# Scores of the chunked linear attention: one matmul per head on its own 32 rows and PSUM bank, in place of block-diagonal queries

## Chip, cores and metric

One core of a Trainium2 chip runs the whole program. The metric is device time in microseconds (us) of one execution; lower is better. Three executions of the kernel before gave 1266.64, 1267.24 and 1271.37 us, median 1267.24 us.

## The reference, cut to what matters

Two token groups (512 prompt tokens, 1024 sample tokens) go through one layer: modulated RMSNorm, an input projection, four mixers side by side, a gate, an output projection, a norm and a residual add. The change lies in one mixer, the gated linear attention (GLA) with 4 heads of 32 key columns and 64 value columns, run forwards and backwards:

```python
def gla_chunked(q, k, v, g, strict):
    # o_t = sum_{s<=t} (q_t * prod_{r=s+1..t} a_r) . k_s  v_s,  a = exp(g), per head
    ...
    decay = jnp.exp(jnp.where(mask[:, :, None], diff, -jnp.inf))
    scores = jnp.einsum('bhtd,bhsd,bhtsd->bhts', qi, ki, decay)
    intra = jnp.einsum('bhts,bhsv->bhtv', scores, vi)
    ...

o_f = gla_chunked(q, k, v, log_gate(lr_f, wg2_f, bg_f), strict=False)
o_b = flip(gla_chunked(flip(q), flip(k), flip(v), flip(log_gate(lr_b, wg2_b, bg_b)), strict=True))
o = rms_norm(o_f + o_b, onorm_g)
```

All is float32 to a tight tolerance, so a product of two operands is taken as three matmuls on the parts high and low of each (h*h, h*l, l*h), in the type float32r.

## The kernel before, in words

The 1536 tokens are three groups of 512: group 2 is the prompt, groups 0 and 1 the sample. For each group `jobs` runs the input projection as many matmuls over weights that stream in (SyncE queue), are split into a high part on ScalarE (ACT, L259) and a low part on GpSimd (POOL, L83), and are used by TensorE (PE) into the PSUM tiles `ps_mm`. These projections, the gate path and the output projection are given a late priority (`later`), and the scheduler of the tile framework, which fixes the order of every engine's instructions when the program is built, places them between the work of the mixers. So the order on each engine follows from priorities and from the scheduler's own estimate of durations; no table in the kernel sets it, and on the chip it is fixed.

`gla_pass1` (L711 to L838) runs once for each group, with tokens along the free dimension and the 4 x 32 key columns on the 128 partitions. The scores within 128 tokens are built by levels m = 1, 2, 4, ..., 64: at level m, pairs of neighbouring runs of m tokens see each other, with queries (`qsi`, `qpi`) and keys (`ksx`, `kpx`) that carry the decay up to that level, so after each level those four tiles are multiplied by decay products (L86, on POOL and VectorE (DVE)). For the six levels above 1, `level` (L746) casts the keys to `kh` (ACT, L751) with the rest `kl` (POOL, L83), and the queries to `qh` (ACT, L757) with the rest `ql` (DVE, L83).

One matmul of 128 x 128 keys against the queries would sum over all four heads. So the kernel before spreads the queries block-diagonally: the tiles `qb` [128, 2 blocks, 4 heads, 128 tokens] are zero but for the head's own 32 rows, are zeroed once per group (L740), and at each level 16 copies of 32 x 256 elements fill them (8 of `qh` on ACT at L764, 8 of `ql` on DVE at L765; half of each for the first pair of blocks). Then each block of 128 tokens takes three matmuls of 512 columns (called at L771, recorded at the helper's line L80) into one of three `ps_s` banks, and DVE copies what the level's mask selects into `st` (COPY_PREDICATED of 128x512, L774; at m = 64 four copies on ACT, L776 and L777). `st` is [tokens, block, head, tokens].

After the levels, `st` is split into `sth` (ACT, L815) and `stl` (DVE, L83), and its matmuls with the values (L820, L821) and the state products follow. Over the three groups the spread is 144 copies on ACT and 144 on DVE.

The same row-group form of matmul already stands in the kernel once: the Fourier mixer has two matmuls over 32 rows (`alt` with `um`) in a chain of matmuls over 128 rows, and `ada_cols` has matmuls over 4 rows (L172).

Of the kernel before, what the change touches and what calls it, by code (L numbers as in the profile page):

```python
# [43 lines left out]
def hybrid_encoder(  # L44
# [24 lines left out]
    def ps_s(dt=F32):  # L69
        return ps.tile([128, 512], dt, tag="s", bufs=3, name="ps_s")  # L70
# [7 lines left out]
    def mms(out, terms, first=True, last=True, skip=False):  # L78
        for i, (a, b) in enumerate(terms):
            T.matmul(out, a, b, start=first and i == 0, stop=last and i == len(terms) - 1, skip_group_check=skip)  # L80
# [20 lines left out]
    S.preload_act_table_set("natural_log_exp_and_others")  # L101
    ones = const.tile([128, 128], F32, name="ones")
    V.memset(ones, 1.0)
    zero = const.tile([128, 1], F32, name="zero")
    V.memset(zero, 0.0)
    eps = const.tile([128, 1], F32, name="eps")
    V.memset(eps, EPS)

# [602 lines left out]
    def gla_pass1(pool, ppool, g, blk0, ap_all, u_f, u_b, aq, ak, vhl, ff, avx):  # L711

        qpi = ppool.tile([128, 512], F32, tag=f"qpi{g}", bufs=1, name=f"qpi{g}")
        qsi = ppool.tile([128, 512], F32, tag=f"qsi{g}", bufs=1, name=f"qsi{g}")
        ksx = pool.tile([128, 512], F32, tag="ksx", bufs=1, name="ksx")
        mul(V, qpi, aq, ff[0])
        mul(V, qsi, aq, ff[1])

        prod = pool.tile([128, 512], F32, tag="kpx", bufs=1, name="prod2")
        for i, src in enumerate((qsi, qpi)):  # L720
            qv, kv, pv = (t.rearrange("p (n two) -> p two n", two=2) for t in (src, ak, prod))
            mul(G, pv[:, i], qv[:, i], kv[:, 1 - i])
        pd = ps_o()
        for b in range(4):
            T.matmul(pd[:, 4 * b:4 * b + 4], prod[:, b * 128:(b + 1) * 128], hm, start=True, stop=True)
        own = sm.tile([128, 16], F32, tag="own", bufs=2, name="own2")
        S.copy(own, pd[:, 0:16])
        avx = avx.rearrange("p b (h d) -> p (b h) d", h=4)
        mul(V, avx, avx, own.unsqueeze(2).to_broadcast([128, 16, 64]))
        o4 = ap_all[:, blk0:blk0 + 4, :].rearrange("p b (h d) -> p (b h) d", h=4)  # L730
        add(V, o4, o4, avx)
        kpx = pool.tile([128, 512], F32, tag="kpx", bufs=1, name="kpx")
        st = pool.tile([128, 4, 4, 128], F32, tag="st", bufs=1, name="st")
        G.memset(st, 0.0)
        tf, tb = ff
        ntot = 512

        qb = [[pool.tile([128, 2, 4, 128], F32R, tag=f"qb{k}{u}", bufs=1, name="qb") for k in "hl"] for u in range(2)]
        for t in (*qb[0], *qb[1]):
            V.tensor_copy(t.rearrange("p b h t -> p (b h t)"), zero.to_broadcast([128, 1024]))  # L740

        def halves(t, m):
            v = t.rearrange("p (n two m) -> p n two m", two=2, m=m)
            return v[:, :, 0, :], v[:, :, 1, :]

        def level(li, m):  # L746
            kh = pool.tile([128, 512], F32R, tag="kh", bufs=2, name="kh")
            kl = pool.tile([128, 512], F32R, tag="kl", bufs=2, name="kl")
            for i, src in enumerate((ksx, kpx)):
                s_, h_, l_ = halves(src, m)[i], halves(kh, m)[i], halves(kl, m)[i]  # L750
                S.copy(h_, s_)  # L751
                sub(G, l_, s_, h_)
            qh = pool.tile([128, 512], F32, tag="qh", bufs=2, name="qh")
            ql = pool.tile([128, 512], F32, tag="ql", bufs=2, name="ql")
            for i, src in enumerate((qsi, qpi)):
                s_, h_, l_ = halves(src, m)[i], halves(qh, m)[i], halves(ql, m)[i]
                S.copy(halves(qh.bitcast(F32R), m)[i], s_)  # L757
                sub(V, l_, s_, h_)
            for u in range(2):
                uc = slice(u * 256, (u + 1) * 256)  # L760
                qbh, qbl = qb[u]
                for h in range(4):
                    r = slice(32 * h, 32 * h + 32)
                    S.copy(qbh[r, :, h, :], qh[r, uc].rearrange("p (b t) -> p b t", b=2))  # L764
                    V.tensor_copy(qbl[r, :, h, :], ql[r, uc].rearrange("p (b t) -> p b t", b=2))  # L765
                for i in range(2):
                    b = 2 * u + i
                    c = slice(b * 128, (b + 1) * 128)
                    pt = ps_s()
                    rh, rl = qbh[:, i].rearrange("p h t -> p (h t)"), qbl[:, i].rearrange("p h t -> p (h t)")  # L770
                    mms(pt, [(kh[:, c], rh), (kh[:, c], rl), (kl[:, c], rh)])  # L771
                    ptv = pt.rearrange("p (h t) -> p h t", h=4)
                    if m < 64:
                        V.copy_predicated(st[:, b], mk[:, li - 1, :].unsqueeze(1).to_broadcast([128, 4, 128]), ptv)  # L774
                    else:
                        S.copy(st[0:64, b, :, 64:128], ptv[0:64, :, 64:128])  # L776
                        S.copy(st[64:128, b, :, 0:64], ptv[64:128, :, 0:64])  # L777

        for li, m in enumerate(LEVELS):
            if m > 1:  # L780
                level(li, m)
            n2 = ntot // 2
            tfv, tbv = (t.rearrange("p (n two) -> p n two", two=2) for t in (tf, tb))

            def bc(t, i):
                return t[:, :, i].unsqueeze(2).to_broadcast([128, n2, m])

            q1, q2 = halves(qpi, m)
            mul(G, q2, q2, bc(tfv, 0))
            q1, q2 = halves(qsi, m)  # L790
            mul(G, q1, q1, bc(tbv, 1))
            if m == 1:
                k1, k2 = halves(ak, 1)
                mul(G, halves(ksx, 1)[0], k1, bc(tfv, 1))
                V.tensor_copy(halves(ksx, 1)[1], k2)
                V.tensor_copy(halves(kpx, 1)[0], k1)
                mul(G, halves(kpx, 1)[1], k2, bc(tbv, 0))
            else:
                k1, k2 = halves(ksx, m)
                mul(V, k1, k1, bc(tfv, 1))  # L800
                k1, k2 = halves(kpx, m)
                mul(V, k2, k2, bc(tbv, 0))
            ntf = pool.tile([128, n2], F32, tag=f"tf{n2}", bufs=1, name="ntf")
            ntb = pool.tile([128, n2], F32, tag=f"tb{n2}", bufs=1, name="ntb")
            mul(V, ntf, tfv[:, :, 0], tfv[:, :, 1])
            mul(V, ntb, tbv[:, :, 0], tbv[:, :, 1])
            tf, tb, ntot = ntf, ntb, n2
        tfin = ppool.tile([128, 2, 4], F32, tag=f"tfin{g}", bufs=1, name=f"tfin{g}")
        V.tensor_copy(tfin[:, 0, :], tf)
        V.tensor_copy(tfin[:, 1, :], tb)  # L810
        for b in range(4):
            c = slice(b * 128, (b + 1) * 128)
            sth = pool.tile([128, 4, 128], F32R, tag="kh", bufs=2, name="sth")
            stl = pool.tile([128, 4, 128], F32R, tag="kl", bufs=2, name="stl")
            S.copy(sth, st[:, b])  # L815
            sub(V, stl, st[:, b], sth)
            po = ps_o()
            pov = po.rearrange("p (h t d) -> p h t d", h=4, t=2)
            for h in range(4):
                T.matmul(pov[:, h], sth[:, h, :], vhl[:, b, h], start=True, stop=False)  # L820
                T.matmul(pov[:, h, 0, :], stl[:, h, :], vhl[:, b, h, 0, :], start=False, stop=True)  # L821
            o4 = ap_all[:, blk0 + b, :].rearrange("p (h d) -> p h d", h=4)
            for t in range(2):
                add(V, o4, pov[:, :, t, :], o4)
            for src, u in ((ksx, u_f), (kpx, u_b)):
                pt = ps_t()
                T.transpose(pt[:, 0:128], src[:, c], ident)
                kth = pool.tile([128, 128], F32R, tag="kth", bufs=2, name="kth")
                ktl = pool.tile([128, 128], F32R, tag="ktl", bufs=2, name="ktl")
                S.copy(kth, pt[:, 0:128])  # L830
                sub(V, ktl, pt[:, 0:128], kth)
                pu = ps_o()
                puv = pu[:, 0:256].rearrange("p (h d) -> p h d", h=4)
                mms(puv, [(kth, vhl[:, b, :, 0, :]), (kth, vhl[:, b, :, 1, :]), (ktl, vhl[:, b, :, 0, :])])
                for h in range(4):
                    r = slice(32 * h, 32 * h + 32)
                    S.copy(u[r, blk0 + b, :], puv[r, h, :])
        return qpi, qsi, tfin  # L838
# [521 lines left out]
```

## Time and profile before

| | us |
|---|---|
| median of 3 executions | 1267.24 |
| the profiled execution's own time | 1264.35 |
| its span, first to last instruction | 1262.5 |
| PE busy | 1115.4 (88%) |
| DVE busy | 878.2 (70%) |
| ACT busy | 723.1 (57%) |
| POOL busy | 555.3 (44%) |
| mean granted TensorE clock | 0.943 |

The profiled execution is one of its own and not one of the three. What is said per instruction or per stretch comes from it. Matmuls are pipelined, with ends that are modelled, so the time a matmul costs in a row of matmuls is read from the distance of two starts, not from its duration.

### The profile page before, as it was taken

To read this page: it belongs to the slowest core of one execution; us is meant where nothing else is said; L and a number is where in the kernel's file an instruction comes from. 1 tells how busy PE (TensorE), PEld (TensorE's weight loads), DVE (VectorE), ACT (ScalarE), POOL (GpSimd) and SP (SyncE) were. 2 spreads that over 40 slices of the span, in tenths; PEclk is the share of its full clock that TensorE was granted. 3 is DMA by queue.
4 is the path that set the end of the run, shared out by engine and by line. 5 is a ranking of instruction groups with operands and counts; after the bars stand their busy time and mean duration, and the time that the engine had idled before them with its cause. 6 is when DMAs were issued, how large, how long until landed. Compare 5 with 4: busy or idle time off the path is not lost. (4 is left out here: it accounts for less than half of the span.)

```text
span 1262.5 us, 20723 instructions
## 1 busy us (share of the span) xinstructions
PE 1115.4 (88%) x7258; PEld 977.6 (77%) x7258; DVE 878.2 (70%) x1618; ACT 723.1 (57%) x1752; POOL 555.3 (44%) x503
## 2 busy tenths in 40 slices
PE   5998798899999958898997779859999998988995
PEld 1587697685999946667897758758988987987995
DVE  6469988638443699854359996485787678787536
ACT  4354667547665437674224567634666777776653
POOL 3256536734233487334526654455242321333123
PEclk8998999889999978899998989969999999997998
DMA  8371424456223613255653123455235212145133
GB/s 311 105 221 51 143 67 136 147 186 191 79 68 95 214 43 123 65 185 177 176 163 117 51 67 125 142 167 179 73 112 198 84 59 74 45 137 164 51 110 116
DMA packets 111224, 158.43 MB, mean 125 GB/s; under 512 B 11749, under 2 KB 58309, under 8 KB 111121
## 3 DMA queue, kind: packets, MB, share of 16 engines
q1 hardware_dynamic: 110824, 157.10, 39.7%
q8 instruction: 57, 0.93, 0.3%
q14 instruction: 47, 0.38, 0.1%
q10 hardware_dynamic: 296, 0.01, 0.0%
HBM read 125.22 MB, written 31.86 MB: 124 GB/s over the span
## 5 line engine op out<-in xcount | busy, mean ns | idle before, releaser
L83 POOL TENSOR_TENSOR wl<-wr,wh 128x512 fp32r<-128x512 f32 (+1 forms) x199 | 267.1, 1346 | 397.4 <-ACT wh L259 336.0
L80 PE MATMUL ps_mm<-wl,oph 128*128 128x256 f32 x1120 | 323.9, 290 | 9.0 <-POOL wl L83 6.3
L80 PE MATMUL ps_mm<-wh,oph 128*128 128x256 f32 x1120 | 321.8, 290 | 9.7 <-ACT kev L449 4.9
L80 PE MATMUL ps_mm<-wh,opl 128*128 128x256 f32 x1120 | 321.5, 289 | 0.0
L80 PEld LDWEIGHTS ps_mm<-wl,oph 128*128 128x128 f32 x1120 | 219.5, 196 | 13.2 <-POOL wl L83 7.3
L80 PEld LDWEIGHTS ps_mm<-wh,oph 128*128 128x128 f32 x1120 | 217.6, 195 | 15.4 <-ACT kev L449 5.2
L80 PEld LDWEIGHTS ps_mm<-wh,opl 128*128 128x128 f32 x1120 | 218.7, 196 | 2.7
L259 ACT CAST wh<-wr 128x512 fp32r<-128x512 f32 (+1 forms) x216 | 131.7, 612 | 125.6 <-PE ps_mm L80 68.6
L503 DVE TENSOR_REDUCE nm<-ps_s 128x1 f32<-128x512 f32 x160 | 108.6, 685 | 56.7 <-PE ps_s L502 55.8
L83 DVE TENSOR_TENSOR ptl<-ps_t,pth 128x512 fp32r<-128x512 f32 x160 | 107.9, 683 | 46.7 <-ACT pth L520 46.2
L80 PE MATMUL ps_mm<-oph,wh 128*128 128x512 f32 x288 | 119.6, 416 | 18.8 <-ACT cev L458 10.2
L510 ACT ACTIVATE pr<-ps_s,nm 128x512 f32<-128x512 f32 x160 | 109.4, 690 | 25.5 <-DVE nm L506 25.0
L80 PE MATMUL ps_mm<-opl,wh 128*128 128x512 f32 x288 | 117.0, 406 | 0.0
L80 PE MATMUL ps_mm<-oph,wl 128*128 128x512 f32 x288 | 116.9, 407 | 0.0
L520 ACT CAST pth<-ps_t 128x512 fp32r<-128x512 f32 x160 | 91.3, 590 | 43.7 <-PE ps_t L518 42.5
L518 PE MATMUL ps_t<-cs,pr 128*128 128x128 f32 x640 | 92.3, 278 | 2.4 <-ACT pr L510 1.1
L518 PEld LDWEIGHTS ps_t<-cs,pr 128*128 128x128 f32 x640 | 76.0, 143 | 12.5 <-ACT pr L510 2.9
L765 DVE CAST qb<-ql 32x256 fp32r<-32x256 f32 x144 | 81.1, 563 | 2.9 <-PE ps_s L80 0.8
L80 PEld LDWEIGHTS ps_mm<-oph,wh 128*128 128x128 f32 x288 | 57.0, 198 | 33.2 <-ACT cev L458 11.6
L80 PE MATMUL ps_s<-qb,kh 128*128 128x512 f32 x144 | 50.2, 441 | 27.0 <-DVE st L774 22.7
L80 PEld LDWEIGHTS ps_mm<-oph,wl 128*128 128x128 f32 x288 | 56.7, 197 | 12.4
L80 PEld LDWEIGHTS ps_mm<-opl,wh 128*128 128x128 f32 x288 | 57.4, 199 | 11.5
(350 smaller groups left out, 2373.2 us busy)
## 6 DMA issues: line engine op xcount, KB each, us to landing
wr<-wp SPq DMA_DIRECT2D x152, 256.0 KB, 2.8
wr<-wo SPq DMA_DIRECT2D x60, 256.0 KB, 2.7
adar<-ada SPq DMA_DIRECT2D x16, 512.0 KB, 6.6
zT<-zr SPq DMA_DIRECT2D x30, 256.0 KB, 2.3
zt<-zT SPq DMA_DIRECT2D x30, 256.0 KB, 4.1
mt<-mixd SPq DMA_DIRECT2D x24, 256.0 KB, 4.3
xt<-x_s SPq DMA_DIRECT2D x4, 1024.0 KB, 5.5
wr<-ada SPq DMA_DIRECT2D x16, 256.0 KB, 2.8
```

Source lines behind the costliest of these rows:

```text
L80: T.matmul(out, a, b, start=first and i == 0, stop=last and i == len(terms) - 1, skip_group_check=skip)
L83: e.tensor_tensor(out, a, b, ALU.subtract)
L259: (V.tensor_copy if part_engine(HIGH_V, u, S) is V else S.copy)(h[:, 0:n], raw[:, 0:n])
L503: V.tensor_reduce(nm[:, f:f + 1], sp, AX, ALU.max, negate=True)
L510: S.activation(pr, sps[f], AF.Exp, bias=nm[:, 0:1], accum_out=rsum[:, b, h, f:f + 1])
L518: T.transpose(pt[:, k * 128:(k + 1) * 128], pr[f][:, k * 128:(k + 1) * 128], ident)
L520: S.copy(pth[f][:, :, qc], ptv)
L765: V.tensor_copy(qbl[r, :, h, :], ql[r, uc].rearrange("p (b t) -> p b t", b=2))
```

## The change

The tiles `qb`, their zeroing and all copies into them go, with the constant `zero`. `qh` and `ql` become float32r. For each of the 4 blocks and 3 terms there are now four matmuls, one for each head, of 32 rows (the head's own), 128 key columns and 128 query columns; head h writes all four blocks into its own PSUM bank: three from `ps_s` and the fourth from `ps_o`, which shares its three banks with the transposes. `st` is now ordered [tokens, head, block, tokens], so that the copy out of PSUM is one per head, of the same 128x512, and the split of `st` reads it with a stride.

```diff
-    zero = const.tile([128, 1], F32, name="zero")
-    V.memset(zero, 0.0)
...
-        qb = [[pool.tile([128, 2, 4, 128], F32R, tag=f"qb{k}{u}", bufs=1, name="qb") for k in "hl"] for u in range(2)]
-        for t in (*qb[0], *qb[1]):
-            V.tensor_copy(t.rearrange("p b h t -> p (b h t)"), zero.to_broadcast([128, 1024]))
...
-            qh = pool.tile([128, 512], F32, tag="qh", bufs=2, name="qh")
-            ql = pool.tile([128, 512], F32, tag="ql", bufs=2, name="ql")
+            qh = pool.tile([128, 512], F32R, tag="qh", bufs=2, name="qh")
+            ql = pool.tile([128, 512], F32R, tag="ql", bufs=2, name="ql")
...
-            for u in range(2):
-                uc = slice(u * 256, (u + 1) * 256)
-                qbh, qbl = qb[u]
-                for h in range(4):
-                    r = slice(32 * h, 32 * h + 32)
-                    S.copy(qbh[r, :, h, :], qh[r, uc].rearrange("p (b t) -> p b t", b=2))
-                    V.tensor_copy(qbl[r, :, h, :], ql[r, uc].rearrange("p (b t) -> p b t", b=2))
-                for i in range(2):
-                    b = 2 * u + i
-                    c = slice(b * 128, (b + 1) * 128)
-                    pt = ps_s()
-                    rh, rl = qbh[:, i].rearrange("p h t -> p (h t)"), qbl[:, i].rearrange("p h t -> p (h t)")
-                    mms(pt, [(kh[:, c], rh), (kh[:, c], rl), (kl[:, c], rh)])
-                    ptv = pt.rearrange("p (h t) -> p h t", h=4)
-                    if m < 64:
-                        V.copy_predicated(st[:, b], mk[:, li - 1, :].unsqueeze(1).to_broadcast([128, 4, 128]), ptv)
...
+            pts = [ps_s(), ps_s(), ps_s(), ps_o()]
+            for b in range(4):
+                c = slice(b * 128, (b + 1) * 128)
+                for i, (k, q) in enumerate(((kh, qh), (kh, ql), (kl, qh))):
+                    for h in range(4):
+                        r = slice(32 * h, 32 * h + 32)
+                        T.matmul(pts[h][:, c], k[r, c], q[r, c], start=i == 0, stop=i == 2)
+            for h in range(4):
+                ptv = pts[h].rearrange("p (b t) -> p b t", b=4)
+                if m < 64:
+                    V.copy_predicated(st[:, h], mk[:, li - 1, :].unsqueeze(1).to_broadcast([128, 4, 128]), ptv)
...
-            S.copy(sth, st[:, b])
-            sub(V, stl, st[:, b], sth)
+            S.copy(sth, st[:, :, b])
+            sub(V, stl, st[:, :, b], sth)
```

In the changed file the line numbers are lower by two to ten (the level's matmul is L760, its predicated copy L764). The scheduler orders the changed program anew, so other work moves too. The built programs show how, at two places.

PE, group 2, around one block's matmuls in the middle of the levels, before (`ps_s<-qb,...` is the level, `ps_mm<-...` the projections):

```order
L80 MATMUL ps_s<-qb,kh 128x512 [waits DVE_49]
L80 MATMUL ps_s<-qb,kh 128x512
L80 MATMUL ps_s<-qb,kl 128x512
L80 MATMUL ps_mm<-wl,oph 128x256
L80 MATMUL ps_mm<-wh,opl 128x256
L80 MATMUL ps_mm<-wh,oph 128x256
```

Four more projection matmuls follow before the next block's three.

PE, group 2, the end of one level and the fourth head of the next, as it stands now (x3 are the heads 0, 1 and 2 in turn; `ps_o` is head 3):

```order
L760 MATMUL ps_s<-qh,kh 128x128 x3
L760 MATMUL ps_s<-ql,kh 128x128 x3
L760 MATMUL ps_s<-qh,kl 128x128 x3
L760 MATMUL ps_o<-qh,kh 128x128 [waits Activation_49]
L760 MATMUL ps_o<-ql,kh 128x128 [waits DVE_49]
L760 MATMUL ps_o<-qh,kl 128x128 [waits Pool_49]
```

Head 3 comes first, as 12 matmuls on one row group; then stand 8 projection matmuls, then for heads 0, 1 and 2 three matmuls each that wait for DVE (their bank's copy of the level before), then 27 in turn over three heads. Between the levels there were some 30 projection matmuls per level in group 2, and there are 8 now; those that left stand after the levels.

DVE, group 0, before, four rows of the spread and what stands around them:

```order
L774 COPY_PREDICATED st<-mk,ps_s 128x512 [waits PE_49]
L774 COPY_PREDICATED st<-mk,ps_s 128x512 [waits DVE_49,PE_49]
L765 CAST qb<-ql 32x2x128 [waits DVE_49,PE_49]
L765 CAST qb<-ql 32x2x128 x3
L774 COPY_PREDICATED st<-mk,ps_s 128x512 [waits PE_49]
L86 TENSOR_TENSOR ksx<-ksx,ntf 128x16x16 [waits Pool_49]
L86 TENSOR_TENSOR kpx<-kpx,ntb 128x16x16 [waits Pool_49]
L83 TENSOR_TENSOR ql<-qsi_7107,qh 128x8x32 [waits DVE_49,Activation_49]
```

and now, at a later level of the same group (`cev`, `ropess`, `rs_*` belong to the rotary step of the attention queries, L342 to L366; `rp_t` is made by POOL from `cev`):

```order
L348 TENSOR_REDUCE ropess<-rp_t_3246 128x8 [waits Activation_49]
L113 TENSOR_SCALAR rs_v<-ropess 128x8 [waits DVE_49]
L115 SCALAR_TENSOR_TENSOR rs_a<-rs_y 128x8 [waits Activation_49]
L86 TENSOR_TENSOR rs_b<-rs_a,rs_v 128x8 [waits DVE_49]
L119 SCALAR_TENSOR_TENSOR rs_r<-rs_b,rs_y 128x8 [waits DVE_49]
L86 TENSOR_TENSOR cev<-cev,rs_r 128x512 [waits DMAHW5_49,DMAHW1_49,DVE_49]
L86 TENSOR_TENSOR cev<-cev,rope_118 128x512 [waits DVE_49,Pool_49]
L89 TENSOR_TENSOR cev<-cev,rp_t_3246 128x512 [waits DVE_49]
L764 COPY_PREDICATED st<-mk,ps_s 128x512 [waits PE_49] x3
L83 TENSOR_TENSOR ql<-qsi_7217,qh 128x4x64 [waits Activation_49]
```

The copies into `qb` are gone, the four predicated copies of a level stand together (head 3's ahead of this piece), and in two levels each of groups 0 and 1 a whole rotary step stands between head 3's copy and the copies of heads 0 to 2.

## Rows read from the trace of the kernel before

**Rows 1.** The page's part 1: busy time, share, instructions of each engine.
```profile
PE 1115.4 (88%) x7258; PEld 977.6 (77%) x7258; DVE 878.2 (70%) x1618; ACT 723.1 (57%) x1752; POOL 555.3 (44%) x503
```
**Rows 2.** Windows, all engines, over the three GLA stretches; last columns clock, DMA, GB/s.
```profile
98.70:167.70 69.00, 54.78 (x340) 49.63 (x339) 67.58 (x133) 39.07 (x97) 39.05 (x39) 0.90 0.30 95
442.70:532.70 90.00, 68.89 (x280) 54.55 (x281) 88.79 (x159) 56.41 (x135) 59.74 (x57) 0.85 0.25 77
676.30:769.50 93.20, 73.60 (x410) 62.76 (x409) 89.64 (x163) 53.70 (x133) 57.85 (x60) 0.91 0.24 73
```
**Rows 3.** Groups by line, DVE: xcount, busy us, mean ns, idle before and its releaser.
```profile
L765 DVE CAST qb<-ql 32x256 fp32r<-32x256 f32 x144 | 81.1, 563 | 2.9 <-PE ps_s L80 0.8
L774 DVE COPY_PREDICATED st<-mk,ps_s 128x512 f32<-128x512 uint8 x60 | 42.3, 730 | 1.1 <-PE ps_s L80 0.3
...
L740 DVE CAST qb<-zero 128x1024 fp32r<-128x1024 f32 x12 | 14.7, 1284 | 9.0 <-DMA mixd<-oc 8.9
...
L86 DVE TENSOR_TENSOR kpx<-kpx,ntb 128x256 f32<-128x256 f32 x18 | 12.5, 697 | 0.0
...
L83 DVE TENSOR_TENSOR ql<-qsi,qh 128x256 f32<-128x256 f32 x18 | 9.8, 543 | 0.0
...
L86 DVE TENSOR_TENSOR ksx<-ksx,ntf 128x256 f32<-128x256 f32 x18 | 8.0, 442 | 0.0
```
**Rows 4.** Who waited for whom, PE: us in total, times, longest us.
```profile
PE ps_s L80 <- DVE st L774: 22.7, 12, 3.9
```
**Rows 5.** Timeline, PE, in the levels of group 2: start, duration, instructions merged.
```profile
130.80 0.62 PE L80 MATMUL ps_s<-qb,kl 128*128 128x512 f32 x2
131.25 0.28 PE L80 MATMUL ps_mm<-wl,oph 128*128 128x256 f32 x1
131.37 0.27 PE L80 MATMUL ps_mm<-wh,opl 128*128 128x256 f32 x1
```
**Rows 6.** Timeline, PE, of 128x128 weights with few moving columns (L820, L821).
```profile
172.87 0.30 PE L820 MATMUL ps_o<-vhl,sth 128*128 128x128 f32 x1
173.01 0.24 PE L821 MATMUL ps_o<-vhl,stl 128*128 128x64 f32 x1
173.09 0.31 PE L820 MATMUL ps_o<-vhl,sth 128*128 128x128 f32 x1
```
**Rows 7.** Timeline, PE, transposes through `rc`, and the matmul behind them.
```profile
308.10 0.46 PE L488 MATMUL ps_t<-rc,q 128*128 128x128 f32 x4
308.39 0.41 PE L624 MATMUL ps_mm<-opl,wlr 128*64 128x512 f32 x1
```
**Rows 8.** Timeline, PE, two matmuls over 32 rows between matmuls over 128 rows.
```profile
620.88 0.28 PE L80 MATMUL ps_s<-tabh,eo 128*128 128x258 f32 x1
621.09 0.51 PE L80 MATMUL ps_s<-alt,um 32*128 32x258 f32 x2
621.53 0.39 PE L80 MATMUL ps_s<-tabl,eo 128*128 128x258 f32 x1
621.75 0.28 PE L80 MATMUL ps_s<-tabh,eo 128*128 128x258 f32 x1
```
**Rows 9.** Groups by line: one rotary pass on POOL, one on DVE.
```profile
L86 POOL TENSOR_TENSOR rp_t<-cev,rope 128x256 f32<-128x256 f32 x24 | 24.3, 1029 | 13.4 <-DVE cev L86 9.4 <-DVE rs_v L115 2.4 <-DVE rs_r L121 1.0
...
L86 DVE TENSOR_TENSOR cev<-cev,rs_r 128x512 f32<-128x512 f32 x12 | 11.5, 957 | 0.1
```
**Rows 10.** Windows, all engines, behind the last GLA stretch.
```profile
820.00:830.00 10.00, 1.56 (x8) 1.09 (x8) 9.96 (x22) 3.20 (x7) 5.60 (x9) 0.60 0.24 76
830.00:840.00 10.00, 3.44 (x19) 2.99 (x20) 7.67 (x16) 2.37 (x6) 4.05 (x8) 0.50 0.95 294
```
**Rows 11.** Windows, all engines, inside the stretch of group 0.
```profile
460.00:480.00 20.00, 15.52 (x50) 11.90 (x51) 19.76 (x29) 11.05 (x26) 15.76 (x13) 0.74 0.22 66
```
**Rows 12.** Timeline, PE, the same 32-row pair as in rows 8, earlier.
```profile
253.54 0.79 PE L80 MATMUL ps_s<-alt,um 32*128 32x258 f32 x2
254.26 0.58 PE L80 MATMUL ps_s<-tabl,eo 128*128 128x258 f32 x1
```

More of the change, by code (lines that the diff above doesn't have):

```diff
@@ L752, in level @@
                 sub(G, l_, s_, h_)
-            qh = pool.tile([128, 512], F32, tag="qh", bufs=2, name="qh")
-            ql = pool.tile([128, 512], F32, tag="ql", bufs=2, name="ql")
+            qh = pool.tile([128, 512], F32R, tag="qh", bufs=2, name="qh")
+            ql = pool.tile([128, 512], F32R, tag="ql", bufs=2, name="ql")
             for i, src in enumerate((qsi, qpi)):
                 s_, h_, l_ = halves(src, m)[i], halves(qh, m)[i], halves(ql, m)[i]
-                S.copy(halves(qh.bitcast(F32R), m)[i], s_)
+                S.copy(h_, s_)
@@ L758, in level @@
                 sub(V, l_, s_, h_)
-            for u in range(2):
-                uc = slice(u * 256, (u + 1) * 256)
-                qbh, qbl = qb[u]
-                for h in range(4):
-                    r = slice(32 * h, 32 * h + 32)
-                    S.copy(qbh[r, :, h, :], qh[r, uc].rearrange("p (b t) -> p b t", b=2))
-                    V.tensor_copy(qbl[r, :, h, :], ql[r, uc].rearrange("p (b t) -> p b t", b=2))
-                for i in range(2):
-                    b = 2 * u + i
-                    c = slice(b * 128, (b + 1) * 128)
-                    pt = ps_s()
-                    rh, rl = qbh[:, i].rearrange("p h t -> p (h t)"), qbl[:, i].rearrange("p h t -> p (h t)")
-                    mms(pt, [(kh[:, c], rh), (kh[:, c], rl), (kl[:, c], rh)])
-                    ptv = pt.rearrange("p (h t) -> p h t", h=4)
-                    if m < 64:
-                        V.copy_predicated(st[:, b], mk[:, li - 1, :].unsqueeze(1).to_broadcast([128, 4, 128]), ptv)
-                    else:
-                        S.copy(st[0:64, b, :, 64:128], ptv[0:64, :, 64:128])
-                        S.copy(st[64:128, b, :, 0:64], ptv[64:128, :, 0:64])
+            pts = [ps_s(), ps_s(), ps_s(), ps_o()]
@@ new lines, in level @@
+            for b in range(4):
[8 more added lines that the diff above has]
+                    V.copy_predicated(st[:, h], mk[:, li - 1, :].unsqueeze(1).to_broadcast([128, 4, 128]), ptv)
+                else:
+                    S.copy(st[0:64, h, :, 64:128], ptv[0:64, :, 64:128])
+                    S.copy(st[64:128, h, :, 0:64], ptv[64:128, :, 0:64])
```

## The prediction

> **What bounds the kernel now.** I read the page's busy shares first. PE is busy 88% of the span, DVE 70% [rows 1]. An average over stages says little, so I looked next at the stretches of the change. I count each from the group's first query multiplication on DVE (it makes `qpi` from `aq` and begins at 98.7, 442.7 and 676.3 us) to the end of its last predicated copy. The three last 69.0, 90.0 and 93.2 us, 252.2 in all [rows 2]. There the reader is to see DVE busy for 67.6, 88.8 and 89.6 us, almost without a gap, while PE stands idle for 14, 21 and 20 us. So DVE sets the pace here, and the list of waits agrees: PE's longest item is the level's matmul waiting for the predicated copy that frees its bank, 22.7 us [rows 4]. Outside these stretches PE is mostly full. PE runs in a fixed order and is filled with projections, so DVE time saved here is worth only what PE then does sooner: **the end moves by PE's idle time, and by PE's own work.**
>
> **What leaves DVE and ACT.** The spread is 144 copies on DVE, 81.1 us with a mean of 563 ns [rows 3], all but one inside the stretches. ACT loses as many, but ACT is busy 39, 56 and 54 us of the three stretches [rows 2], so I cost those at nothing; the cover is DVE's longer queue, and once that is gone ACT's remaining casts still fit. The zeroing of `qb` is 14.7 us on DVE, before the stretches [rows 3]. Much of it lies where DVE waits for loads anyway; I take 4 us of it (ends 0 and 14.7).
>
> **What a level costs DVE after the change.** Two `ql` of 0.54, one `ksx` of 0.44, one `kpx` of 0.70 and four predicated copies of 0.73 [rows 3]: 1.09 + 0.44 + 0.70 + 2.92 = 5.15 us.
>
> **What a level costs PE.** Before, 12 matmuls of 512 columns, two of which start 0.45 us before the next one, so 0.225 each [rows 5]: 2.7 us. Now there are 48 of 128 columns. No row before shows two matmuls on different row groups, so their price needs bounds. From above: a matmul of 128 or 64 columns behind a weight load of 128 columns, two in 0.22 us, so 0.11 each [rows 6]. From below: four transposes, each with its own load, in 0.29 us, 0.073 each [rows 7], and if four row groups really ran at once, 0.11/4 = 0.028 (an estimate). By the order, 12 matmuls of a level are on head 3's rows and 9 come three by three on one row group, so I take 0.11 for these 21; for the 27 that go round three heads I take 0.073, since each then finds a load on other rows ahead of it, and the transposes are the nearest row where the load is not the limit. 21 x 0.11 + 27 x 0.073 = 4.3 us.
>
> The Trainium skill's page "TensorEngine Tiling (Array Packing)" (section Key Properties) goes further: different tiles execute weight loads and matmuls in parallel. By it all 27 would cost near the lowest bound, a level would need 3.1 us, and DVE alone would set the pace; no run here shows it.
>
> Going from 128-row to 32-row matmuls has a price of its own. The last 128-row matmul ends at 620.88 + 0.28 = 621.16, the pair over 32 rows at 621.60, the next 128-row one at 621.92 [rows 8]: 0.44 for two and 0.32 for one, where such matmuls otherwise follow at 0.12. That is about 0.20 for each switch, either way. In the new order each level is one or two runs of its own, 21 runs over the program, so a level pays 0.39. With its 8 projection matmuls at 0.12 [rows 5] PE's period is 4.3 + 0.39 + 0.95 = 5.6 us, half a microsecond over DVE's 5.15. The new levels are about balanced, PE just ahead.
>
> **The stretches after.** DVE's work there was 246 us, the sum of the three windows [rows 2]. Minus 81 of spread. Minus about 15 of other work which the new order puts behind the stretches: 8 rotary passes at 0.96 [rows 9], and 16 smaller ones (gates, diagonals, the chunk gate), which I price at the copy's 0.73 as an estimate, with 6 passes of keys coming in at about half a rotary pass: 7.7 + 11.7 - 2.9 = 16.5, rounded down since some are shorter. That leaves 150. Added waits: 15 periods x 0.5 for PE, 7 us. In four levels a rotary step now stands ahead of three predicated copies; it waits for two passes of POOL at 1.03 [rows 9] and for ACT's two short steps, 2.5 us each (an estimate from those rows), 10 us, and the PE's next level, behind those copies, waits with it. Three starts of some 3 us until both casts of the first level are there, 9 us. Sum 150 + 7 + 10 + 9 = 176, so **the stretches shrink by 76 us.**
>
> **What they push out.** PE did more than levels there. Counted in the built order from `prod2` to the last level matmul, the other matmuls were 239, 195 and 279 in the three groups; now they are 93, 137 and 152. At 0.118 for 256 columns and 0.23 for 512 [rows 5] that is 112.6 us before and 46.4 now. **66 us of projections must run elsewhere.** If PE is full there, all 66 come back; that is what I take. Ends: 66, and 30 if they fall where PE idles (PE's idle time outside the stretches is 147 - 55 = 92 us by rows 1 and 2).
>
> The split of `st` reads the same elements with a stride of 128-element runs: I cost it at nothing, with the predicated copies' own strides as the row. The fourth bank taken from `ps_o` is one of three that transposes share; in the stretches few transposes run, so nothing either, up to 3 us.
>
> **Sum.** -76 + 66 - 4 = -14 us against the profiled execution's own 1264.35, which gives 1250. The median of the runs shown lies 2.9 us above that execution, so **1253 us**.
>
> **The rivals.**
>
> *The loads do not overlap (about no change).* The 48 matmuls cost 0.11 each whatever row they are on. For it: the pair over 32 rows takes 0.44 with its switch of 0.20, so 0.24 for two, the 0.12 of matmuls over 128 rows [rows 8]: a matmul over fewer rows is not cheaper by itself. Against: that pair is on one row group, and no row has different ones. PE's period is then 5.3 + 0.39 + 0.95 = 6.6, 1.0 us more in 15 periods: -14 + 15 = +1, **1268 us**. The Trainium skill's "TensorE: Matmul & The Clock Gate" (section LDWEIGHTS) has the rule behind this: the load's time goes by its columns, not by the rows that it fills, which speaks against the change.
>
> *PE becomes slow in the levels (slower).* With 30 fewer projections between levels, PE has holes while the rotary steps hold the copies, and the granted clock falls. It stood at 0.74 in a stretch in which PE was busy 15.5 of 20 us [rows 11]. At the lower level, 1.2 GHz, the 32-row pair with its switch took 0.72 us instead of 0.44 [rows 8, 12], 1.65 times. A level that loads at 0.11 x 1.65 = 0.18 needs 8.7, with the rest 11 us, 4.4 over the serial period. Five of the 15 periods like that give +22 on top of the serial case: **1290 us**. It decides from a mean period of 5.6 + (14 + 6.3)/15 = 7.0 us, a mean price of 0.118 per matmul at 1.34 us for the rest.
>
> *The pushed-out projections fall into holes (much faster).* Behind the last stretch PE is busy 1.6 and 3.4 of two times 10 us, at clock 0.60 and 0.50 [rows 10]. If 25 of the 66 us land in such places: **1228 us**. Against: kv's preparation needs the projections of group 1 first, and those are among the ones pushed out.
>
> **How the numbers follow.** My forecast (partly overlapping loads) gets 0.40, the serial loads 0.25, the low clock 0.15, the filled holes 0.20. A change under 0.5% (6.3 us) cannot be told from none here, so between 1261 and 1273.5 counts as the same. Faster: the filled holes, three quarters of the forecast's own spread (its ends are the 4 us of zeroing, 10 of rotary waits and 7 of price), 0.20 + 0.30 = 0.50. Same: 0.08 of the forecast and 0.16 of the serial case, 0.24. Slower: the low clock, the serial case's upper part and a rest, 0.26. The range takes in the filled holes and the serial case whole and ends just below the low clock's price: 1228 to 1288. The likeliest case alone spans 1240 to 1264.
>
> **What would show it.** Right: the rows of L765, L764 and L740 are gone; the three stretches sum to 165 to 190 us; in the levels DVE and PE are both busy above nine tenths; matmuls that go round the heads start less than 0.09 us apart, those on one row group 0.11. The loads' rival: all start 0.11 apart and PE never idles in the levels. The clock's rival: PEclk below 0.8 in the level windows, and PE waiting for the predicated copy behind a rotary step for 5 us or more at a time. The holes' rival: the stretch behind the last GLA group loses its idle 15 us. My forecast is wrong if the stretches shrink by less than 50 us, or if much less than 60 us of projections come back behind them.

## The result, and the profile after

The changed kernel takes 1280.69 us (median of 6 runs, 1275.62 to 1283.56), the kernel before 1267.59 beside it: ratio 1.0095, 95% interval 1.0067 to 1.0123. The forecast was 1253, faster; it is **13 us slower**, inside the range (1228 to 1288), on the side that had 0.26. The profiled execution took 1283.56 us with a span of 1281.8; it is the slowest of the six, and that of before, 1264.35, lies below all of its own, so the two profiles differ by 19 us and the medians by 13.

The page's part 1 of the changed kernel, against [rows 1]:

```profile
PE 1158.3 (90%) x7906; PEld 1028.9 (80%) x7906; DVE 797.8 (62%) x1461; ACT 667.1 (52%) x1608; POOL 554.4 (43%) x503
```

DVE's busy time fell by 80 us. The spread and the zeroing that went were 96 [rows 3]; some of DVE's other instructions became longer, such as the multiplication of `ksx`, 0.76 us each where it was 0.44. PE's idle time fell from 147 to 123 us (span less busy), but PE's busy time rose by 43. Net 19 us of span.

Windows over the three stretches (from the query multiplication to the last predicated copy; columns as in [rows 2], the clock third from the end):

```profile
97.80:150.20 52.40, 47.48 (x394) 45.32 (x394) 45.54 (x78) 14.44 (x37) 34.23 (x34) 0.65 0.14 41
424.60:489.60 65.00, 53.21 (x440) 50.27 (x438) 59.79 (x97) 19.01 (x53) 45.25 (x48) 0.71 0.22 66
696.30:772.30 76.00, 63.32 (x495) 57.89 (x493) 67.19 (x115) 24.63 (x65) 52.02 (x54) 0.71 0.21 63
```

The stretches shrank from 252.2 to 193.4 us, by 59. The clock column is what to look at: 0.65, 0.71, 0.71 where it was 0.90, 0.85, 0.91. A closer look inside group 2's levels, five microseconds each, first before, then after:

```profile
135.00:140.00 5.00, 3.94 (x23) 2.99 (x22) 4.97 (x10) 2.98 (x8) 3.29 (x5) 1.00 0.32 107
140.00:145.00 5.00, 5.00 (x39) 4.74 (x38) 4.86 (x13) 2.33 (x6) 0.71 (x1) 1.00 0.72 241
```

```profile
135.00:140.00 5.00, 5.00 (x38) 4.66 (x35) 4.77 (x8) 1.94 (x5) 3.91 (x5) 0.50 0.02 5
140.00:145.00 5.00, 5.00 (x43) 4.88 (x42) 3.30 (x7) 1.32 (x4) 2.77 (x5) 0.50 0.19 52
```

Before, PE had holes in the first of the two (3.94 of 5 us busy) and was granted 1.00 in both; now it is busy without a gap and is granted 0.50, which is 1.2 GHz. This low stretch begins at 123.7 us, behind a hole of 1.63 us on PE (120.76 to 122.39), and lasts 37.5 us, for the first 33 of which PE has no gap. The timeline of PE over one such level (start, duration, merged count) shows what it was busy with:

```profile
140.64 0.47 PE L760 MATMUL ps_o<-qh,kh 32*128 32x128 f32 x1
140.83 0.43 PE L760 MATMUL ps_s<-qh,kh 32*128 32x128 f32 x3
...
142.84 0.41 PE L760 MATMUL ps_o<-ql,kh 32*128 32x128 f32 x1
143.05 0.41 PE L760 MATMUL ps_o<-qh,kl 32*128 32x128 f32 x1
143.39 0.58 PE L80 MATMUL ps_mm<-wh,opl 128*128 128x256 f32 x1
143.77 0.41 PE L80 MATMUL ps_mm<-wh,oph 128*128 128x256 f32 x1
143.98 0.41 PE L80 MATMUL ps_mm<-wl,oph 128*128 128x256 f32 x1
...
145.40 0.49 PE L760 MATMUL ps_s<-qh,kh 32*128 32x128 f32 x3
145.67 0.43 PE L760 MATMUL ps_s<-ql,kh 32*128 32x128 f32 x3
145.88 0.43 PE L760 MATMUL ps_s<-qh,kl 32*128 32x128 f32 x3
...
147.19 0.47 PE L760 MATMUL ps_o<-qh,kh 32*128 32x128 f32 x1
```

Head 3's matmuls (`ps_o`) follow each other at 0.21 us; the heads 0, 1 and 2 start three at a time (x3), and the next three come 0.21 later. In this level that holds for all 36 of them, also for the first nine (145.40 to 145.88), which the order puts three by three on one row group. Head 3 of the next level starts at 147.19, so the period is 6.55 us. So row groups do run side by side, and every step costs 0.21 where [rows 6] had 0.11. The projections pay it too: 256 columns at 0.21 where [rows 5] had 0.12.

PE's list of waits has this in the place of [rows 4]:

```profile
PE ps_s L760 <- DVE st L764: 9.8, 6, 3.5
```

The longest of these is the rotary step that the new order puts ahead of the copies (timelines of DVE and PE, idle time in brackets):

```profile
480.81 1.19 DVE L86 TENSOR_TENSOR cev<-cev,rope 128x512 f32<-128x512 f32 x1 [1.82 <-POOL rp_t L86]
482.04 1.09 DVE L89 TENSOR_TENSOR cev<-cev,rp_t 128x512 f32<-128x512 f32 x1
483.06 1.92 DVE L764 COPY_PREDICATED st<-mk,ps_s 128x512 f32<-128x512 uint8 x3
```

```profile
483.82 0.47 PE L760 MATMUL ps_s<-qh,kh 32*128 32x128 f32 x1 [3.45 <-DVE st L764]
```

The hole behind the last group, [rows 10], shrank and did not vanish: from 820 to 840 PE is now busy 13.7 us (before 5.0), but from there to 880 only 33 of 40 (before 37):

```profile
820.00:840.00 20.00, 13.73 (x67) 11.25 (x65) 13.24 (x24) 12.54 (x30) 13.40 (x15) 0.84 0.55 172
```

**Theory after the comparison:** the saving on DVE is real, and the loss is PE's. The scheduler's order lets matmuls over 32 rows run alone or three at a time, TensorE is granted 1.2 GHz in that part, and all PE work there costs about double. Rivals: the steps in a row cost by themselves, at any clock; the pushed-out projections eat the saving whatever PE's price.

### The profile page after: what moved, and what is told of

The parts are those of the page before. It is cut to its first block, busy times and chain, and to the rows that moved or that the text cites. A ratio compares the mean times of both kernels' runs of the same rounds, so it can differ in the third digit from the quotient of the medians.

```text
span 1281.8 us, 21661 instructions
## 1 busy us (share of the span) xinstructions
PE 1158.3 (90%) x7906; PEld 1028.9 (80%) x7906; DVE 797.8 (62%) x1461; ACT 667.1 (52%) x1608; POOL 554.4 (43%) x503
## 5 line engine op out<-in xcount | busy, mean ns | idle before, releaser
L80 PE MATMUL ps_mm<-wh,oph 128*128 128x256 f32 x1120 | 329.3, 297 | 12.3 <-ACT cev L456 8.0
L80 PE MATMUL ps_mm<-wl,oph 128*128 128x256 f32 x1120 | 333.3, 298 | 6.8 <-POOL wl L83 5.7
L80 PE MATMUL ps_mm<-wh,opl 128*128 128x256 f32 x1120 | 330.1, 296 | 0.0
L80 PEld LDWEIGHTS ps_mm<-wh,oph 128*128 128x128 f32 x1120 | 224.8, 202 | 18.4 <-ACT cev L456 8.4
L80 PEld LDWEIGHTS ps_mm<-wl,oph 128*128 128x128 f32 x1120 | 226.8, 202 | 11.5 <-POOL wl L83 6.8
L80 PEld LDWEIGHTS ps_mm<-wh,opl 128*128 128x128 f32 x1120 | 226.7, 203 | 2.1
L499 PE MATMUL ps_s<-kT,qT 128*128 128x512 f32 x128 | 56.5, 441 | 2.9 <-ACT pr L508 2.8
L83 POOL TENSOR_TENSOR opl<-m,oph 128x512 fp32r<-128x512 f32 x30 | 39.5, 1334 | 28.1 <-ACT oph L1030 27.9
```

What stands on the lines that cost most here:

```text
L83: e.tensor_tensor(out, a, b, ALU.subtract)
L499: T.matmul(sp, qT[:, h, qc], kT[kv][:, kc], start=True, stop=False)
```

## The experiments

All ratios are against the kernel before, run on the same chip (1265 us in all three sittings). Each run is built anew, so the scheduler also places the other work anew. On PE this shows as the number of other matmuls, mostly projections, from one level to the next: 7 or 8 for most levels of the changed kernel and of run 5, 10 to 17 in run 1, 7 to 15 in run 6, about 20 in run 2, and none in runs 7 and 8 (for most levels each, counted in PE's timelines).

**1. Full rows.** In the level, of the changed kernel:

```diff
-T.matmul(pts[h][:, c], k[r, c], q[r, c], start=i == 0, stop=i == 2)
+T.matmul(pts[h][:, c], k[:, c], q[:, c], start=i == 0, stop=i == 2)
```

> Each of the 48 matmuls of a level contracts over all 128 rows instead of its head's 32 (so the scores of the four heads are summed, which is not the computation); number, columns, banks and copies stay. Theory (clock): the 32-row matmuls are what the granted clock falls for. Then the clock in the levels comes back to 0.85 or more, a matmul costs 0.11 us, a level 48 x 0.11 + 0.95 = 6.2 us instead of about 7, and the time falls by some 10 to 15 us, to 1262 to 1272. Rival (order): what costs is the matmuls that run alone, on one row group. Then nothing runs side by side any more, 48 slots stand in the place of 30 at the same 0.21 us, and the time rises by 15 x 18 x 0.21 = 57 us, to over 1330.

1264.48 us, ratio 0.9975 (0.9950 to 1.0001). Windows of its stretches:

```profile
98.40:157.10 58.70, 54.08 (x415) 53.47 (x414) 45.77 (x80) 15.76 (x38) 35.48 (x35) 0.88 0.15 46
426.40:500.90 74.50, 63.10 (x478) 60.25 (x479) 68.87 (x119) 30.20 (x76) 57.28 (x57) 0.91 0.25 77
677.50:753.50 76.00, 67.38 (x516) 64.47 (x515) 70.74 (x116) 27.63 (x70) 54.27 (x56) 0.93 0.23 68
```

The clock is back, and the kernel is some 15 us faster than the changed one (1.2% by the two ratios) although nothing runs side by side any more. The clock's price is larger than what the row groups save in this order.

**2. Rotate over four heads.** The same matmuls, kept in program order on PE:

```diff
-T.matmul(pts[h][:, c], k[r, c], q[r, c], start=i == 0, stop=i == 2)
+mm = T.matmul(pts[h][:, c], k[r, c], q[r, c], start=i == 0, stop=i == 2)
+tc.stamp_issue_order_token(mm.ins if hasattr(mm, 'ins') else mm, 'levels')
```

> The level's matmuls keep program order on PE, so that they go round the four heads (0123 twelve times) instead of head 3 alone first; nothing else. By both theories 12 slots stand in the place of 30. If the slots that ran alone are the cost (rival, order), the clock is back at 0.85 or more in the levels, the period is DVE's, 5.2 to 5.7 us, and the time is 1235 to 1250. If 32-row matmuls hold the clock down in any order (theory, clock), the level windows still show 0.5 to 0.65, a slot takes 0.21, 12 of them 2.6 us and eight projection matmuls 1.7, the period is 5.5 to 6 us and the time 1255 to 1268.

1226.65 us, ratio **0.9687 (0.9652 to 0.9721)**: faster than both kernels, below either expectation. Page, windows of the stretches, and the timeline of one level with the projections on both sides:

```profile
PE 1098.3 (90%) x7906; PEld 967.6 (79%) x7906; DVE 801.8 (66%) x1461; ACT 667.3 (55%) x1608; POOL 558.5 (46%) x503
```

```profile
97.30:148.30 51.00, 42.07 (x433) 39.19 (x431) 47.12 (x82) 15.78 (x38) 36.86 (x36) 0.80 0.33 104
407.30:486.60 79.30, 61.40 (x499) 52.70 (x500) 71.72 (x120) 32.11 (x79) 60.02 (x59) 0.81 0.27 82
652.60:731.00 78.40, 64.54 (x538) 55.61 (x537) 70.71 (x117) 29.57 (x73) 59.31 (x59) 0.87 0.26 77
```

```profile
132.21 0.28 PE L80 MATMUL ps_mm<-wh,opl 128*128 128x256 f32 x1
132.43 0.33 PE L760 MATMUL ps_s<-qh,kh 32*128 32x128 f32 x3
132.44 0.32 PE L760 MATMUL ps_o<-qh,kh 32*128 32x128 f32 x1
132.59 0.28 PE L760 MATMUL ps_s<-ql,kh 32*128 32x128 f32 x3
132.60 0.27 PE L760 MATMUL ps_o<-ql,kh 32*128 32x128 f32 x1
...
133.71 0.28 PE L760 MATMUL ps_s<-qh,kl 32*128 32x128 f32 x3
133.72 0.27 PE L760 MATMUL ps_o<-qh,kl 32*128 32x128 f32 x1
133.91 0.50 PE L80 MATMUL ps_mm<-vhl,wsh 128*128 128x256 f32 x2
```

Four heads start within 0.01 us of each other, and the whole level of 48 shown here goes from 132.43 to 133.72, 1.3 us: 0.027 each. The clock is 0.80 to 0.87 over the stretches, so 32 rows as such don't take it down. Whether the rotation holds it up, or the 20 or so projections that now stand between two levels, this run does not separate. The stretches sum to 208.7 us, longer than the changed kernel's 193.4, and the kernel is 52 us faster by the two ratios: PE's busy time is 60 us less. A stretch's length is a poor yardstick when other work may move in and out of it.

**3. No spread, the old matmuls** (the kernel before without spread and zeroing):

```diff
-mms(pt, [(kh[:, c], rh), (kh[:, c], rl), (kl[:, c], rh)])
+mms(pt, [(kh[:, c], qh), (kh[:, c], ql), (kl[:, c], qh)])
```

> The kernel before, with its 12 matmuls of 512 columns over 128 rows a level, but without spread and zeroing: the right side is all of qh or ql (the scores are not those of the reference). This is the DVE and ACT saving alone, without any new price on PE. Theory (clock): all of the loss is on PE; here the clock stays at 0.85 or more, the three stretches shrink by 80 to 95 us, the projections come back with some 66, and the time is 1240 to 1252. Rival (pushed-out work): the DVE time saved is worth nothing, since what PE did beside it has to run elsewhere; then the time is 1262 to 1270 here too.

1221.72 us, ratio 0.9652 (0.9621 to 0.9682). The saving on DVE and ACT alone is worth 44 us, more than expected: the rival of the pushed-out work falls, and my sum had the saving too low as well. The rotation (2) gets within 5 us of this.

**4. One product of three:**

```diff
-for i, (k, q) in enumerate(((kh, qh), (kh, ql), (kl, qh))):
+for i, (k, q) in enumerate(((kh, qh),)):
```

> Of the three products of a level only the first is made (16 matmuls of 32 rows instead of 48; the corrections for the low parts are left out); DVE, ACT and POOL do what they did. Theory (PE's price at the low clock sets the period): PE's level shrinks by two thirds, DVE's 5.15 us set the period, and the time falls by 15 x 1.7 = 25 us, to 1250 to 1260; with fewer of them the clock in the levels is 0.6 to 0.8. Rival (waits between DVE, POOL and PE set the period, not PE's work): the time moves by less than 6 us.

1222.01 us, ratio 0.9645 (0.9608 to 0.9682), some 57 us under the changed kernel, over twice what was expected. With a third of the level's matmuls the loss is gone: it is PE's work, not a wait.

**5 and 6. The changed kernel's order by hand, and its lone matmuls over 128 rows.** Run 5 writes the order out (with the token of run 2); run 6 adds the last change to it:

```diff
+solo = [(3, b, i) for b in range(4) for i in range(3)] + [(h, 0, i) for h in range(3) for i in range(3)]
+for n, (h, b, i) in enumerate(solo + [(h, b, i) for b in range(1, 4) for i in range(3) for h in range(3)]):
...
-r = slice(32 * h, 32 * h + 32)
+r = slice(32 * h, 32 * h + 32) if n >= 21 else slice(0, 128)
```

> Control for the next run: the order that the changed kernel has in most levels (head 3's 12 matmuls, nine of the other heads each behind its own head's, 27 that go round three heads) is written out and kept by hand; same work. Both theories: the time of the changed kernel within 8 us (1270 to 1290) and a granted clock of 0.50 to 0.65 in the level windows.

> The order of the control; only the 21 matmuls of a level that run alone contract over all 128 rows instead of 32 (so their scores sum four heads, which is not the computation), the 27 that go round three heads stay on 32 rows. The number of slots in a row is the same 30. Theory (what runs alone on 32 rows takes the clock down, and the clock is the cost): the level windows come back to 0.8 or more, the 30 slots take 3.3 us instead of 6.4, and the time is 1235 to 1255. Rival (the 30 slots in a row cost by themselves, the low clock only goes with them): the time stays within 8 us of the control, 1270 to 1290. Second rival (any 32-row matmul takes the clock down): the windows stay below 0.65.

Run 5: 1271.72 us, ratio 1.0044 (1.0021 to 1.0068). Run 6: 1255.36, ratio 0.9921 (0.9893 to 0.9949), at the upper end of what was expected. Windows of the stretches, run 5, then run 6:

```profile
97.20:150.60 53.40, 46.30 (x387) 44.03 (x386) 45.68 (x78) 14.29 (x37) 34.23 (x34) 0.67 0.14 41
426.70:501.10 74.40, 58.71 (x450) 51.82 (x449) 65.00 (x118) 26.86 (x66) 51.36 (x54) 0.70 0.20 59
677.90:754.50 76.60, 64.22 (x495) 58.39 (x493) 65.34 (x115) 24.63 (x65) 50.41 (x54) 0.73 0.21 63
```

```profile
97.40:147.50 50.10, 44.89 (x417) 43.60 (x416) 45.46 (x81) 15.98 (x39) 35.56 (x35) 0.86 0.18 54
417.00:499.50 82.50, 64.68 (x485) 58.40 (x486) 68.97 (x119) 29.87 (x76) 58.26 (x57) 0.81 0.23 69
672.60:748.20 75.60, 64.88 (x516) 59.82 (x514) 68.97 (x116) 26.71 (x69) 53.36 (x56) 0.89 0.22 64
```

The order of the level's matmuls is the same, only what the 21 contract over differs: the clock goes from about 0.70 to 0.85 and the time falls by 16 us. The plainest view of it is one window in the same level of group 2, run 5, then run 6, with 8 projections in that level and PE full in both:

```profile
130.00:135.00 5.00, 5.00 (x48) 4.66 (x50) 3.77 (x7) 0.73 (x2) 3.61 (x4) 0.50 0.00 0
130.00:135.00 5.00, 5.00 (x69) 4.79 (x66) 4.59 (x8) 1.38 (x5) 2.95 (x4) 1.00 0.19 52
```

The rival that steps in a row cost the same at any clock falls. Run 5 is also the control of run 2, since it keeps its order by the same token: 45 us lie between the two, by the order of the level's matmuls and by what the scheduler then puts between the levels. Its profiled execution took 1261.01 us, the fastest of its twelve and 11 under their median, so its rows, here and in the table further down, show it at its best; run 6's took 1257.78. The control is 6 us faster than the changed kernel by the ratios: that much is not the order of the level's matmuls, but how the rest of the program was scheduled around it.

**7 and 8. Two heads at a time, one at a time,** in program order with the token:

```diff
+for h, b, i in [(h, b, i) for p in (0, 2) for b in range(4) for i in range(3) for h in (p, p + 1)]:
...
+for h, b, i in [(h, b, i) for h in range(4) for b in range(4) for i in range(3)]:
```

(the first line is run 7's loop over the level's matmuls, the second run 8's).

> Program order kept, with heads 0 and 1 going round first (24 matmuls), then 2 and 3: two row groups side by side, 24 slots a level, no projections between the levels in the built order. Theory (the clock goes by how many row groups work side by side): with two of four it lies between one and four; if it holds (0.85 or more), a level is 24 x 0.11 = 2.6 us, DVE's 5.15 sets the period and the time is 1225 to 1245; if it falls to 0.5, 24 x 0.21 = 5.1 us, the period about 5.5 to 6, and the time 1245 to 1265. Rival (only matmuls quite alone take it down): the first of the two.

> Program order kept, each head's 12 matmuls by themselves: one row group at a time in all 48. Theory (lone 32-row matmuls take the clock down): 0.5 through the whole of the levels, 48 x 0.21 = 10.2 us a level, 4 us more than the control in 18 levels, 1340 to 1370. Rival (the clock falls for the holes that PE has while it waits for copies, not for the rows): PE has no holes left here, so the clock stays at 0.85 or more, a level is 48 x 0.11 = 5.3 us, and the time is 1255 to 1275.

Run 7: 1257.38 us, ratio 0.9937 (0.9915 to 0.9959). Run 8: 1287.82, ratio 1.0192 (1.0153 to 1.0230). Windows of 5 us in the levels, run 7 (group 2), then run 8 (group 1):

```profile
135.00:140.00 5.00, 5.00 (x60) 5.00 (x58) 4.53 (x10) 1.02 (x4) 2.57 (x5) 0.50 0.02 5
140.00:145.00 5.00, 4.88 (x50) 4.54 (x48) 5.00 (x10) 0.44 (x2) 2.47 (x4) 0.50 0.00 0
```

```profile
735.00:740.00 5.00, 5.00 (x56) 4.93 (x57) 3.79 (x6) 0.41 (x1) 2.63 (x4) 1.00 0.03 12
740.00:745.00 5.00, 5.00 (x33) 4.78 (x31) 4.64 (x10) 1.54 (x4) 2.88 (x5) 0.50 0.49 145
```

Both are granted the low clock, also with two row groups side by side. In run 8 it falls at 740.0 us, with PE full for the ten microseconds before and for the 41 that it stays low: the rival that holes of PE are needed for it falls. Run 7 still beats the kernel before a little: 24 steps at half clock are cheap enough. So the clock alone does not decide, but steps times the price of a step. Run 8 was expected at 1340 or more and is a miss: its later levels take 6.95 to 7.3 us from first start to last, not 48 x 0.21 = 10.2, because PE starts the next head's matmuls while the last few of the head before are still to come. Here the first of head 3 (`ps_o`) starts ahead of one of head 2 that stands before it in the order:

```profile
759.83 0.47 PE L759 MATMUL ps_o<-qh,kh 32*128 32x128 f32 x1
760.03 0.41 PE L759 MATMUL ps_s<-qh,kh 32*128 32x128 f32 x1
```

**9. Zeroing on POOL,** in the kernel before:

```diff
-V.tensor_copy(t.rearrange("p b h t -> p (b h t)"), zero.to_broadcast([128, 1024]))
+G.memset(t.bitcast(F32), 0.0)
```

> The kernel before, with only the zeroing of qb moved from DVE to POOL (14.7 us of DVE work). It measures the prediction's smallest term alone: 4 us by the prediction (1259 to 1264 where before has 1265.5); by the reading that this work lies where DVE waits for loads anyway, 0 (1264 to 1267); if POOL's own fill delays the start of a stretch, slower (over 1268).

1262.7 us, ratio 0.9985 (0.9967 to 1.0004): 2 us less, between 4 less and none. So the run cannot tell the term of 4 us from nothing; 14.7 it was not.

**10. A cheaper spread in the place of row groups:**

```diff
-    S.copy(qbh[r, :, h, :], qh[r, uc].rearrange("p (b t) -> p b t", b=2))
-    V.tensor_copy(qbl[r, :, h, :], ql[r, uc].rearrange("p (b t) -> p b t", b=2))
+    for i, src in enumerate((qsi, qpi)):
...
+        S.copy(h_, s_)
+        sub(V, l_, s_, h_)
```

> Another way to take DVE work away, without matmuls on row groups: qb is kept, but ACT casts each head's rows straight into it and DVE subtracts straight into it, over all four blocks at once (8 casts and 8 subtractions a level in the place of 2 + 8 and 2 + 8); zeroing on POOL; qb is now one buffer for four blocks. Saved on DVE: 2 x 0.54 us in 18 levels, 19 us, and 14.7 of zeroing. If DVE's work alone sets the pace, 1240 to 1252; if the single buffer makes the casts of a level wait for the last matmul of the one before, 1258 to 1275. The clock in the levels as before, 0.85 or more.

1277.27 us, ratio 1.0102 (1.0077 to 1.0128), slower. Its row of the predicated copy, with the idle time ahead of it, against 1.1 us in [rows 3]:

```profile
L767 DVE COPY_PREDICATED st<-mk,ps_s 128x512 f32<-128x512 uint8 x60 | 41.7, 734 | 24.1 <-PE ps_s L81 22.9 <-POOL st L733 0.9 <-POOL kl L84 0.2
```

DVE has less to do and waits for PE, which waits for the one buffer to be filled (13 us of waits for `qb` before matmuls, 18 before their weight loads). That is the second branch, 2 us beyond its end; that the buffer accounts for all of the loss is not shown.

**11. Rotation, and the level m = 32 copied by ACT:**

```diff
+if m == 32:
+    for a in range(4):
+        o = 32 * (a ^ 1)
+        S.copy(st[32 * a:32 * a + 32, h, :, o:o + 32], ptv[32 * a:32 * a + 32, :, o:o + 32])
-if m < 64:
+elif m < 64:
```

> The rotation over four heads as before, and the level of m = 32 copied out by ACT in 16 strided copies of 32 x 128 instead of four predicated copies on DVE (2.9 us of DVE less in each of the three groups, some 4 us of ACT more). If DVE still sets the pace in that level, 3 to 8 us less than the rotation alone (1219 to 1224 where that has 1226.65); if the level now waits for ACT's copies, or the next for its banks, the same or up to 4 us more (1226 to 1231). The clock in the levels 0.75 to 0.9, as with the rotation alone.

1226.01 us, ratio 0.9685 (0.9661 to 0.9710): the same as run 2. Taking these copies off DVE gains nothing once the rotation is in; whether they no longer set the end, or ACT's copies cost what they free, the run does not tell.

## Why the prediction was wrong

PE's busy time and its idle time (span less busy), from page 1 of each, and the mean granted clock. The clock's part is an estimate: busy time times (1 - clock), summed over windows of 5 us. All in us of one profiled execution each:

| kernel | PE busy | PE idle | clock | clock's part |
|---|---|---|---|---|
| before | 1115.4 | 147.1 | 0.943 | 46 |
| changed | 1158.3 | 123.5 | 0.900 | 101 |
| 1, full rows | 1150.2 | 112.6 | 0.951 | 39 |
| 2, rotate over four | 1098.3 | 124.0 | 0.944 | 45 |
| 3, no spread | 1098.1 | 120.3 | 0.961 | 30 |
| 5, order pinned | 1141.2 | 118.0 | 0.914 | 81 |
| 6, lone ones over 128 rows | 1134.7 | 121.3 | 0.939 | 54 |
| 7, pairs | 1129.5 | 126.5 | 0.924 | 71 |
| 8, singles | 1173.9 | 110.3 | 0.912 | 92 |

Once the spread is gone, idle lies between 110 and 127 everywhere; what tells the kernels apart is PE's own time, from 1098 to 1174. From before to the changed kernel the clock's part rises by 55, more than the whole rise of 43 in PE's busy time. The 56 between the changed kernel and run 2 are nearly all of the 60 by which their busy times differ. Run 1 pays in the other way, for its steps: without the clock's part its busy time is 1111, and 1053 to 1082 in the others.

- **What bounds the kernel** (DVE in the stretches): right. Run 3 takes only DVE and ACT work away and gains 44 us.
- **What a level costs PE: the step that failed.** A level's own matmuls, "21 x 0.11 + 27 x 0.073 = 4.3 us", and PE's period of 5.6 with switches and eight projections were priced at the full clock from [rows 5 to 8]. Measured in an undisturbed level of the changed kernel: a period of 6.55 us at half clock, of which 2.0 go to the projections (143.39 to 145.40; the sum had 0.95) and 4.5 to the level's own matmuls and a switch. Halved, 6.55 is 3.3 (an estimate of the period at the full clock), so the overlap was better than I took it, and run 2's 1.3 us for 48 is the lowest bound of the prediction (0.028 each). Two errors of opposite sign: the overlap understated, the clock missed. In the level's own matmuls they nearly cancel, which is luck; the projections get no overlap and pay the clock in full. The order was known when I wrote; what I did not see is that it decides both.
- **The Trainium skill** was the better guide on the overlap. "TensorEngine Tiling (Array Packing)", Key Properties: different tiles execute loads and matmuls in parallel. Run 2 agrees, with 48 in 1.3 us. The Trainium skill's "TensorE: Matmul & The Clock Gate" (LDWEIGHTS) has it that a load's time goes by columns, not rows. A step on one row group agrees: 0.21 over 32 rows at half clock, as for the projections over 128. It does not keep different row groups apart (four start within 0.01 us in run 2), so the rival built on it is out.
- **The clock's rival** had 0.15, and the right direction for a cause that was only partly right; its 1290 is nearer to the 1281 measured than the forecast. I let the clock fall through holes while PE waits for rotary steps, five levels of 15 (and counted 30 fewer projections between two levels, where some 30 became 8). Its first sign showed (0.65 to 0.71 in the stretches), its second, waits of 5 us behind a rotary step, did not: the longest is 3.5. Each of the three long low stretches of the changed kernel does begin within 4 us of holes on PE (1.6 to 2.4 us in all), so holes may have had a part in the fall. What I did not foresee is that the clock stays low while PE is full, in most levels of all three groups.
- The Trainium skill's "TensorE: Matmul & The Clock Gate", section "HAM oscillation", tells of waits between matmuls that close the gate. Run 8 differs: there it closed without any (5.00 of 5.00 busy on both sides of 740.0, clock 1.00, then 0.50). Runs 1 and 6 show it mostly open where the matmuls contract over 128 rows.
- **The stretches**: 59 us less instead of 76. Fifteen periods that are 0.95 longer would make 14 of the 17 that are missing. The rotary steps were priced too low: the four levels that have one take 9.4 to 11.3 us in place of 6.55, 15 in all where the sum had 10, since the heads then start one by one as well. DVE's own work there is 172.5 us, not 150: 22 other instructions left, about as counted, but a level's instructions came to 5.5 us for 5.15, and others became longer too. PE idles 29 us in the stretches; only 10 of it waits for DVE's copies, most of the rest is projections that wait for their weights or their bank.
- **What they push out**: counted from a stretch's start to its last level matmul at full-clock prices, the other matmuls fell from 129 to 69 us, so 60 moved (forecast 66). Outside, PE's busy time rose by 75 (907 to 982 us). The 15 more are the low clock again: the 5 us windows there lose 44 us to it, before 27. So about 38 of the 55 fall to the clock inside the stretches and 17 outside. Why the clock is low in more places far from the levels is open; run 5 has 29 there and run 2 has 18, so most of it goes with the one schedule.
- **Nothing for `st`'s stride, ACT and the fourth bank**: right as far as it shows. The cast of `st` takes 0.62 us in both, the subtraction 0.69 after 0.68 (medians of 12).
- **A switch** between 128-row and 32-row matmuls, priced at 0.20, costs about 0.1 at the full clock (run 2: 132.21 to 132.43 and 133.72 to 133.91, where 0.11 is normal).
- **The filled holes**: no. Outside the stretches PE's idle time is 94 us, before 92.
- **The signs of being wrong** that the prediction named did not show: the stretches shrank by more than 50 us, and the projections came back. They watch how much work moves, and none watches what a matmul costs where it is.

Run 6, the changed kernel's order with most of the clock back, takes 1255 us. That is next to the 1253 forecast by chance, since the sum had the overlap and the clock both wrong.

## What to carry to other kernels

Row groups pay most while all four work side by side (two at a time still gained 0.6% here, one at a time lost 2%): look at the order in which the engine gets them, since a head whose bank need not wait for a copy, here head 3, runs ahead alone, and pin the order if the scheduler breaks it up (here some 50 us, from 1% slower to 3% faster than before). Read PEclk beside PE's busy share in the stretch itself; a PE that is busy all the time at clock 0.50 is not a PE near its limit, and prices taken at the full clock are half of what will be paid. Judge a stretch by PE's busy and idle time over the whole run, not by its length, when a scheduler can move other work in and out of it.

## What was not expected of the hardware

- A granted clock of 0.50 over more than 25 us in which PE has no gap of over 0.2 us, while it runs 32-row matmuls singly, in pairs or in threes (changed kernel, runs 5, 7, 8); in run 8 it also fell with no gap before it. It was 0.80 and more over the stretches when all four row groups go together with more projections between (run 2) or the lone matmuls contract over 128 rows (runs 1, 6).
- A 32-row matmul of 128 columns alone takes as long as a 128-row one of 256 (0.21 at half clock), but four on different row groups cost as much as one: 0.11 at the full clock.
- PE starts a matmul on a free row group ahead of earlier ones that queue for a busy one: 48 in a row, head by head, took 6.95 us from the first start to the last instead of 10 (run 8).
